# Hybrid trunk on one core: the carried state's product made in whole 128-row matmuls, its decay and the norm sums on VectorE, the last group's scaling moved

## The chip, the core and the metric

The kernel runs on one core of one Trainium2 chip. The time is that of one execution on the device, in microseconds (us). Three runs of the kernel before gave 1942.26, 1942.64 and 1945.34 us; the median, 1942.64 us, is the time that the change is measured against.

## The reference, cut to what matters

One layer of a decoder trunk over 1024 positions and 1024 channels: a normed input is projected, goes through a convolution branch and a state-space branch (SSD), is mixed, and passes a gated feed-forward part. The change lies in the state-space branch, in the norm of the convolution branch and in the order of the work between the two. For a chunk of 128 positions, and for each of 32 heads (8 to a group, 64 channels to a head), the branch computes:

```python
a_cs = cumsum(a)                                   # per head, over the chunk
decay = where(causal, exp(a_cs[l] - a_cs[s]), 0)
y_diag = (C @ B.T * decay) @ xs                    # inside the chunk
y_off  = (C @ carry) * exp(a_cs)                   # from the carried state
carry  = exp(a_cs[-1]) * carry + new_state
y = (y_diag + y_off + x * d_skip) * silu(z)
y = y * rsqrt(mean(y**2) + eps) * norm_w           # over the group's 512 channels
```

The convolution branch ends in a layer norm over 1024 channels (`mean`, then the mean of the squared differences), a scaling and a silu.

## The kernel before, in words

The sequence is taken in two halves of 512 positions (`hh` 0 and 1). Channels lie on the 128 partitions, positions along the free axis. A projection of 128 channels is 24 matmuls of 128x128 weights by 512 positions: eight blocks of the contraction, three products each, because each operand is held as a high and a low part (`project`, `mm3`, lines 189 to 204). ScalarE makes the high part of the weights by a cast (L158), VectorE the low part by a subtraction (L163); in the second half the low part of most weights comes back from memory instead (L160). The weights go through three buffers, so a cast waits for the product that used the buffer three products earlier.

`mixers(hh)` runs four groups `g`. For each group it projects and convolves B, C and x, projects the gate z, makes two products of the convolution branch, and then calls `ssd_group`, whose four chunks `c` are mixed into the projections that come next. A chunk, on its engines:

- SyncE loads `ab`: the eight heads' `a_cs`, each copied to all 128 partitions (L640).
- TensorE transposes x and B and multiplies B by C (L646 to L650).
- ScalarE makes the decay (`m`, L653 and L660) and `exp(a_cs)` for all eight heads (`ce`, 128x1024, L663). GpSimd multiplies `ce` by C (L664).
- VectorE masks the product of B and C (`cbm`), scales x to `xs` and `xsd`, and multiplies `m` by `cbm` (L680).
- TensorE adds up, for each head, `xs` times `m` (L685) and the state times `ce` (L688) in one bank `py`; each of these products fills 64 of the 128 output rows, and two heads share the rows. Then it makes the new state `pn` (L693).
- VectorE decays the state and adds the new one (L697, L700), adds the skip term (L703), multiplies by `zs` (L714); ScalarE squares, VectorE sums the squares (L717, L718).

`fill` places taps of a 31-tap convolution (L577, one VectorE instruction each, 480 in all) behind chosen instructions. `scaled()` turns the sum of squares of a finished group into a factor: a TensorE product (L725), a square root (L733), a reciprocal (L734), a small store and a load that copies the row to all partitions, both issued from GpSimd's queue (L736, L737), then four scalings of x (L740). `parts` splits the scaled x into high and low parts (ScalarE L754, VectorE L755). For groups 0 to 2 they are called while the next group is under way; for group 3 they stand inside the gate products `gate_first`, after number 4 of 0 to 7. Then `gated` follows with the eight `gb` products. `held` keeps the four scalings and ties them behind an instruction chosen by hand: the last skip of chunk 0 of the next group, or, for group 3, the low part of the first `gb` weights.

`conv_norm` loads the eight convolved blocks (L862), adds them up on GpSimd (L864, L866), subtracts the mean on VectorE, squares on ScalarE and adds the squares on GpSimd (L876). It runs once beside the `gated` products of the second half, for the first half's data, and once beside the products of `mixed`.

Names in the views: `acc` and `sm` are the two sets of four accumulation banks, `w_*` weights, `st_*` weights as loaded, `c_5`, `c_6` the convolution's sums, `x_1_3` the x of group 3 of the second half, `state_106` the state of group 3.

The order of instructions on each engine is fixed when the program is built: a scheduler places them by priorities and its own timing, and each engine then takes its list strictly in that order.

Of the kernel before, what the change touches and what calls it, by code (L numbers as in the profile page):

```python
# [8 lines left out]
F32 = mybir.dt.float32  # L9
F32R = mybir.dt.float32r  # L10
AF = mybir.ActivationFunctionType
# [52 lines left out]
def kernel(  # L64
# [557 lines left out]
    def ssd_group(pl, hh, g, xT, BT, CT, zs):  # L622
# [10 lines left out]
        for c in range(4):  # L633
# [25 lines left out]
                )  # L659
            exps.append(A.activation(out=m, in_=m, func=AF.Exp, scale=-1.0))  # L660
            if not first:
                ce = pl.tile([P, 8, P], F32, tag="ce", name=f"ce{nm}")
                A.activation(out=ce, in_=ab, func=AF.Exp)  # L663
                G.tensor_tensor(  # L664
                    out=ce, in0=ce, in1=CT[:, cs].unsqueeze(1).to_broadcast([P, 8, P]), op=ALU.mult
                )
            cbm = pl.tile([P, P], F32, tag="cbm", name=f"cbm{nm}")
            V.tensor_mul(cbm, pb[:, P : 2 * P], upper)
# [13 lines left out]
            for i in range(4):  # L682
                pair = [(2 * i + k, py[k * HP : (k + 1) * HP, i * P : (i + 1) * P]) for k in (0, 1)]
                for h, o in pair:
                    TE.matmul(o, xs[:, h * HP : (h + 1) * HP], m[:, h, :], start=True, stop=first)  # L685
                if not first:
                    for h, o in pair:
                        TE.matmul(  # L688
                            o, S[:, h * HP : (h + 1) * HP], ce[:, h, :], start=False, stop=True
                        )  # L690
            if not last:
                pn = bank(0)
                TE.matmul(pn, bt, xsd, start=True, stop=True)  # L693
# [7 lines left out]
            for i in range(4):  # L701
                k = PC_SD + 4 * g + i
                skip = V.scalar_tensor_tensor(  # L703
                    out=xT[:, i, cs],
                    in0=xT[:, i, cs],
                    scalar=pc[:, k : k + 1],
                    in1=py[:, i * P : (i + 1) * P],
                    op0=ALU.mult,
                    op1=ALU.add,
                )  # L710
            fill(FILL[hh][1], skip)
            while held and c == 0:
                issue_after(held.pop(), skip)
            V.tensor_mul(xT[:, :, cs], xT[:, :, cs], zs[:, :, cs])  # L714
            sq = pl.tile([P, 4, P], F32, tag="sq", name=f"sq{nm}")
# [62 lines left out]
    def mixers(hh, hT):  # L778
        pre = first_columns(hh, hT, (CT_B, CT_C, CT_X))
        with pool(f"mixers{hh}") as pl:  # L780
            time_steps(pl, hh, pre[0])
            scaled = parts = None
            for g in range(GROUPS):
                BT = conv4(pl, hh, column(hh, hT, CT_B + g) if g else pre[1], 16 + g)
                CT = conv4(pl, hh, column(hh, hT, CT_C + g) if g else pre[2], 20 + g)
                xT = pl.tile([P, 4, HALF], F32, tag="x4", bufs=2, name=f"x4_{hh}_{g}")
                for i in range(4):
                    j = 4 * g + i
                    conv4(pl, hh, column(hh, hT, CT_X + j) if j else pre[3], j, xT[:, i, :])
                zs = z_gate(pl, hh, hT, g)  # L790
                for i in (2 * g, 2 * g + 1):
                    glu(pl, hh, hT, i)
                    conv31(hh, i)
                if g:
                    scaled()
                if g == 1:
                    yT = big_tile(f"yT{hh}_0")
                if g in (1, 2):
                    parts(yT)
                split_2 = parts  # L800
                scaled, parts = ssd_group(pl, hh, g, xT, BT, CT, zs)
                if g == 3:
                    ssm_out_first(pl, hh, yT)
                    yT = big_tile(f"yT{hh}_2")
                    split_2(yT)
                    gate_first(pl, hh, hT, range(3))
            for j in range(3, 8):
                gate_first(pl, hh, hT, (j,))
                fill(FILL[hh][2], los[-1])
                if j == 4:  # L810
                    scaled()
                    parts(yT)
        return yT

    def gated(pl, hh, hT, yT, during):
# [37 lines left out]
    def conv_norm(pl, hh, place):  # L853

        squares = pl.tile([P, 2, HALF], F32, tag="sq", name=f"csq{hh}")
        stats = pl.tile([P, 2, HALF], F32, tag="stats", name=f"stats{hh}")
        mean, var = stats[:, 0, :], stats[:, 1, :]
        n = 8
        pairs = [pl.tile([P, 2, HALF], F32, tag=f"c{i}", name=f"cc{hh}_{i}") for i in range(n // 2)]
        cs = []  # L860
        for i in range(n):
            G.dma_start(pairs[i // 2][:, i % 2, :], c_scr[hh][i])  # L862
            cs.append(pairs[i // 2][:, i % 2, :])
        G.tensor_add(mean, cs[0], cs[1])  # L864
        for c in cs[2:]:
            G.tensor_add(mean, mean, c)  # L866
        pm = bank(0)
        TE.matmul(pm, mean_w, mean, start=True, stop=True)
        for i, c in enumerate(cs):
            V.tensor_tensor(out=c, in0=c, in1=pm, op=ALU.subtract)  # L870
            if i == 0:
                A.activation(out=var, in_=c, func=AF.Square)
            else:
                sq = squares[:, i % 2, :]
                A.activation(out=sq, in_=c, func=AF.Square)
                G.tensor_add(var, var, sq)  # L876
        return lambda: conv_silu(pl, cs, var, place)

    def conv_silu(pl, cs, var, place):
# [677 lines left out]
```

## Time and profile before

| | before |
|---|---|
| median of three runs | 1942.64 us |
| the profiled execution's own time | 1943.56 us |
| its span in the trace | 1941.9 us |
| TensorE (PE) busy | 1922.9 us, 99% |
| VectorE (DVE) busy | 1617.1 us, 83% |
| ScalarE (ACT) busy | 1099.7 us, 57% |
| GpSimd (POOL) busy | 227.2 us, 12% |

Rows of a timeline give the start in us from the span's start, the length in us, the engine, the line, the operation, what it writes and reads, how many instructions of that kind stand together, and in brackets how long the engine was idle before it and what ended that. Rows of the waits give who waited for whom, the total in us, how often, and the longest. A row of a line gives, behind the colon, the shortest, median and longest duration in ns. Matmuls overlap in the records: each of 512 columns is shown as 0.39 us long, but one starts every 0.23 us, so starts are what to read.

### The profile page before, as it was taken

The page shows a single profiled execution, that of the slowest core. Times are in us where ns is not written, and L with a number is a line of the kernel's source. Part 1 is how long each engine was busy: PE and PEld are TensorE (multiplying, and loading weights), DVE is VectorE, ACT ScalarE, POOL GpSimd, SP SyncE. Part 2 cuts the span into 40 slices and gives each one's busy share as a digit, 9 for nine tenths or more (in the row PEclk, how much of TensorE's full clock was granted, in tenths as well). Part 3 has the DMA queues.
Part 4 walks back from the last instruction along what each step waited for, and adds up shares of the span by engine and source line. Part 5 has one row for each costly group of instructions (what it writes and reads, how often), then busy time and mean ns, then how long its engine had stood idle before and what let it go on. Part 6 is the DMA issues. An engine that isn't in the chain of part 4 may idle for free.

```text
span 1941.9 us, 25994 instructions
## 1 busy us (share of the span) xinstructions
PE 1922.9 (99%) x9424; PEld 1570.9 (81%) x9424; DVE 1617.1 (83%) x2222; ACT 1099.7 (57%) x1628; POOL 227.2 (12%) x275
## 2 busy tenths in 40 slices
PE   9999999999999999999999999999999999999998
PEld 8878888888878888878777888888888888888886
DVE  7488989797998697999978797787788888888778
ACT  6585878654525777776543535365555555553534
POOL 1010011011000111111102250011000000022010
PEclk9999999999999999999999999999999999999999
DMA  6655555547586565564464465766445555479673
GB/s 229 217 193 202 205 201 184 174 160 262 201 286 206 199 215 206 197 217 172 165 226 159 161 229 185 254 250 238 156 163 196 174 178 186 161 275 357 206 245 115
DMA packets 138194, 398.44 MB, mean 205 GB/s; under 512 B 16432, under 2 KB 16976, under 8 KB 138064
## 3 DMA queue, kind: packets, MB, share of 16 engines
q1 hardware_dynamic: 116928, 335.39, 50.1%
q0 software_dynamic: 14656, 49.83, 7.1%
q10 hardware_dynamic: 6480, 11.55, 1.6%
q8 instruction: 74, 1.21, 0.2%
q14 instruction: 56, 0.46, 0.1%
HBM read 300.61 MB, written 96.09 MB: 204 GB/s over the span
## 4 chain that ended last, share of the span: by engine, by line
PE 77%; DVE 9%; issue 7%; DMA 4%; ACT 2%; POOL 1%; SPq 0%; DVEq 0%; POOLq 0%; ACTq 0%
PE acc L194 18%; PE acc L192 17%; PE acc L193 17%; PE sm L192 7%; PE sm L193 7%; PE sm L194 7%; DVE c L577 3%; DVE x L527 1%; PE acc L508 1%; PE sm L685 1%; DMA rstd<-nrm_scr 1%; PE sm L693 1%; ACT m L653 1%; POOL ce L664 1%; DMA w_c<-low_scr 1%
## 5 line engine op out<-in xcount | busy, mean ns | idle before, releaser
L192 PE MATMUL acc<-hT_h,w_c 128*128 128x512 f32 x1000 | 391.8, 392 | 0.0
L194 PE MATMUL acc<-hT_h,w_c 128*128 128x512 f32 x1000 | 390.5, 391 | 0.1
L193 PE MATMUL acc<-hT_l,w_c 128*128 128x512 f32 x1000 | 389.9, 390 | 0.0
L577 DVE SCALAR_TENSOR_TENSOR c<-vl,pc,c 128x512 f32<-128x512 f32 x480 | 374.4, 800 | 8.0 <-ACT c L566 3.6
L192 PEld LDWEIGHTS acc<-hT_h,w_c 128*128 128x128 f32 x1000 | 187.8, 188 | 40.8 <-issue 2.0
L194 PEld LDWEIGHTS acc<-hT_h,w_c 128*128 128x128 f32 x1000 | 187.8, 188 | 40.1 <-issue 0.8
L193 PEld LDWEIGHTS acc<-hT_l,w_c 128*128 128x128 f32 x1000 | 187.8, 188 | 38.9 <-issue 0.6
L158 ACT CAST w_c<-st_c 128x1024 fp32r<-128x1024 f32 x128 | 133.8, 1046 | 148.1 <-PE acc L194 88.5
L664 POOL TENSOR_TENSOR ce<-ce,xbc 128x1024 f32<-128x1024 f32 x28 | 77.7, 2776 | 489.2 <-ACT ce L663 489.2
L1282 ACT CAST w_dn<-dr 128x1024 fp32r<-128x1024 f32 (+1 forms) x72 | 67.1, 942 | 75.3 <-DVE dr L1215 39.6
L163 DVE TENSOR_TENSOR w_c<-st_c,w_c 128x1024 fp32r<-128x1024 f32 x62 | 76.9, 1242 | 36.9 <-ACT w_c L158 36.7
L192 PE MATMUL sm<-h1s,w_s 128*128 128x512 f32 x264 | 102.8, 389 | 0.5 <-ACT fuv L1125 0.5
L193 PE MATMUL sm<-h1s,w_s 128*128 128x512 f32 x264 | 102.7, 389 | 0.0
L194 PE MATMUL sm<-h1s,w_s 128*128 128x512 f32 x264 | 102.2, 389 | 0.0
L653 ACT ACTIVATE m<-ab,acs 128x128 f32<-128x128 f32 x256 | 78.5, 389 | 27.8 <-PE sm L685 26.0
L1283 DVE TENSOR_TENSOR w_dn<-dr,w_dn 128x1024 fp32r<-128x1024 f32 (+1 forms) x72 | 77.7, 1086 | 4.8 <-ACT w_dn L1282 4.6
L527 DVE SCALAR_TENSOR_TENSOR x<-u,pc,x 128x512 f32<-128x512 f32 x96 | 71.0, 753 | 2.7 <-ACT x L525 2.7
L194 PE MATMUL acc<-h1b_h,w_ue 128*128 128x512 f32 x176 | 68.6, 395 | 0.3 <-DVE w_ue L163 0.3
L192 PE MATMUL acc<-h1b_h,w_ue 128*128 128x512 f32 x176 | 68.7, 391 | 0.0
L193 PE MATMUL acc<-h1b_l,w_ue 128*128 128x512 f32 x176 | 68.6, 390 | 0.0
L192 PE MATMUL sm<-h1b_h,w_s 128*128 128x512 f32 x176 | 68.5, 389 | 0.0
L193 PE MATMUL sm<-h1b_l,w_s 128*128 128x512 f32 x176 | 68.5, 389 | 0.0
(369 smaller groups left out, 4592.7 us busy)
## 6 DMA issues: line engine op xcount, KB each, us to landing
st_c<-wcol SPq DMA_DIRECT2D x128, 512.0 KB, 4.5
low_scr<-w_c SPq DMA_DIRECT2D x64, 512.0 KB, 2.9
w_c<-low_scr SPq DMA_DIRECT2D x64, 512.0 KB, 4.4
ab<-acs_scr SPq DMA_DIRECT2D x32, 512.0 KB, 4.0
dr<-wdown SPq DMA_DIRECT2D x55, 256.0 KB, 5.1
st_wo<-wo SPq DMA_DIRECT2D x24, 512.0 KB, 4.1
st_ue<-wup SPq DMA_DIRECT2D x22, 512.0 KB, 3.8
first_scr<-first ACTq DMA_DIRECT2D x44, 256.0 KB, 3.0
```

The lines of the kernel that those rows point to most:

```text
L158: casts.append(A.copy(w[:, 0, :], st))
L163: sub.tensor_tensor(out=w[:, 1, :], in0=st, in1=w[:, 0, :].bitcast(F32), op=ALU.subtract)
L192: TE.matmul(ps, wa(0), xa(0), start=start, stop=False, skip_group_check=more)
L193: TE.matmul(ps, wa(0), xa(1), start=False, stop=False, skip_group_check=more)
L194: TE.matmul(ps, wa(1), xa(0), start=False, stop=stop, skip_group_check=more)
L508: mm = TE.matmul(pss[o][:, ts], ws[o][:, i, k * P : (k + 1) * P], hT[:, j, k, ts], start=n == 0 and k == 0, stop=n == 2 and k == KD - 1,)
L527: V.scalar_tensor_tensor(out=o, in0=u[:, k : k + HALF], scalar=pc[:, wc + k : wc + k + 1], in1=o, op0=ALU.mult, op1=ALU.add,)
L577: step = V.scalar_tensor_tensor(out=c, in0=v[:, k : k + HALF], scalar=pc[:, wc + k : wc + k + 1], in1=c, op0=ALU.mult, op1=ALU.add,)
L653: A.activation(out=m[:, h, :], in_=ab[:, h, :], func=AF.Relu, scale=-1.0, bias=acs[:, c, 8 * g + h : 8 * g + h + 1],)
L664: G.tensor_tensor(out=ce, in0=ce, in1=CT[:, cs].unsqueeze(1).to_broadcast([P, 8, P]), op=ALU.mult)
L1282: A.copy(w[:, 0, cs], src)
L1283: V.tensor_tensor(out=w[:, 1, cs], in0=src, in1=w[:, 0, cs].bitcast(F32), op=ALU.subtract)
```

## The change

1. The carried state's part of a chunk is no longer made head by head with the decay inside the moving operand. Four products of 128 state columns (two heads) by C go to a bank `pq` of their own, early in the chunk; `exp(a_cs)` is made at half the size (128x512, with the even heads' rows on partitions 0 to 63 and the odd heads' on 64 to 127, loaded by two more transfers), and VectorE multiplies `pq` by it. GpSimd's multiplication goes. The skip term takes the result (`ce`) as its addend, and one more VectorE addition brings in `py`.
2. The additions in `conv_norm` (7 for the mean, 7 for the squares, in each of two calls) go from GpSimd to VectorE.
3. For group 3, `scaled()` and `parts` are called two gate products earlier; the scalings of group 2 are tied behind chunk 2 of group 3 and no longer behind chunk 0.

```diff
             if not first:
-                ce = pl.tile([P, 8, P], F32, tag="ce", name=f"ce{nm}")
-                A.activation(out=ce, in_=ab, func=AF.Exp)
-                G.tensor_tensor(
-                    out=ce, in0=ce, in1=CT[:, cs].unsqueeze(1).to_broadcast([P, 8, P]), op=ALU.mult
+                ce = pl.tile([P, 4, P], F32, tag="ce", name=f"ce{nm}")
+                by_two = acs_scr[hh][r : r + 8, :].rearrange("(i k) l -> k i l", k=2)
+                for k in range(2):
+                    SY.dma_start(
+                        ce[k * HP : (k + 1) * HP], by_two[k].partition_broadcast(HP)
+                    )
+                A.activation(out=ce, in_=ce, func=AF.Exp)
+                pq = bank(0)
+                for i in range(4):
+                    TE.matmul(
+                        pq[:, i * P : (i + 1) * P], S[:, i * P : (i + 1) * P], CT[:, cs],
+                        start=True, stop=True,
+                    )
+                V.tensor_tensor(
+                    out=ce, in0=pq.rearrange("p (i l) -> p i l", i=4), in1=ce, op=ALU.mult
                 )
...
-                    TE.matmul(o, xs[:, h * HP : (h + 1) * HP], m[:, h, :], start=True, stop=first)
-                if not first:
-                    for h, o in pair:
-                        TE.matmul(
-                            o, S[:, h * HP : (h + 1) * HP], ce[:, h, :], start=False, stop=True
-                        )
+                    TE.matmul(o, xs[:, h * HP : (h + 1) * HP], m[:, h, :], start=True, stop=True)
...
-                    in1=py[:, i * P : (i + 1) * P],
+                    in1=py[:, i * P : (i + 1) * P] if first else ce[:, i],
...
+            if not first:
+                skip = V.tensor_tensor(
+                    out=xT[:, :, cs],
+                    in0=xT[:, :, cs],
+                    in1=py.rearrange("p (i l) -> p i l", i=4),
+                    op=ALU.add,
+                )
             fill(FILL[hh][1], skip)
-            while held and c == 0:
+            while held and c == (2 if g == 3 else 0):
...
                     gate_first(pl, hh, hT, range(3))
+                    scaled()
+                    parts(yT)
             for j in range(3, 8):
                 gate_first(pl, hh, hT, (j,))
                 fill(FILL[hh][2], los[-1])
-                if j == 4:
-                    scaled()
-                    parts(yT)
...
-        G.tensor_add(mean, cs[0], cs[1])
+        V.tensor_add(mean, cs[0], cs[1])
         for c in cs[2:]:
-            G.tensor_add(mean, mean, c)
+            V.tensor_add(mean, mean, c)
...
-                G.tensor_add(var, var, sq)
+                V.tensor_add(var, var, sq)
```

The lines of the changed kernel that the prediction names: the two loads of `ce` L665, its Exp L668, the products into `pq` L671, the multiplication by the decay L675, `m` times `cbm` L691, the products inside the chunk L696, the state's decay and addition L703 and L706, the skip term L709, the new addition of `py` L718, the scalings L753, the sums of `conv_norm` L876, L878 and L888.

How the instructions stand, at three places. First TensorE in the second half, group 3, chunk 2. Before, from the last two pairs of the chunk's products to the projection that follows:

```order
L685 MATMUL sm_8290<-m_3_2_8268,xs_3_2_8283 64x128 x2
L688 MATMUL sm_8290<-ce_3_2_8278,state_106 64x128 x2
L693 MATMUL sm_8307<-xsd_3_2_8285,bt_3_2_8287 128x512
L646 MATMUL sm_8331<-ident,x_1_3_7667 128x128 x4
L650 MATMUL sm_8336<-xbc_23_7659,xbc_19_7620 128x128
L192 MATMUL acc_8593<-yT_0_h,w_so_6_8590 128x512
```

Now the state's products stand 15 projection matmuls ahead of the others, between matmuls of an earlier projection (`w_so_4`):

```order
L193 MATMUL acc_8527<-yT_0_l,w_so_4_8524 128x512
L194 MATMUL acc_8527<-yT_0_h,w_so_4_8524 128x512
L671 MATMUL sm_8282<-xbc_23_7659,state_106 128x128 x4
L192 MATMUL acc_8527<-yT_0_h,w_so_4_8524 128x512
L193 MATMUL acc_8527<-yT_0_l,w_so_4_8524 128x512
```

and the chunk's own products come in one run, 21 projection matmuls earlier than before (in `w_so_5`, not `w_so_6`):

```order
L194 MATMUL acc_8560<-yT_0_h,w_so_5_8557 128x512
L696 MATMUL sm_8297<-m_3_2_8268,xs_3_2_8290 64x128 x8
L699 MATMUL sm_8306<-xsd_3_2_8292,bt_3_2_8294 128x512
L646 MATMUL sm_8331<-ident,x_1_3_7667 128x128 x4
L650 MATMUL sm_8336<-xbc_23_7659,xbc_19_7620 128x128
L192 MATMUL acc_8560<-yT_0_h,w_so_5_8557 128x512
```

TensorE now meets VectorE twice in a chunk: at L671, which needs the state, and at L696, which needs `m`.

Second, VectorE in the same group, from the state of chunk 1 to `m` of chunk 2. Before:

```order
L697 TENSOR_TENSOR state_106<-state_106,edc 128x512
L703 SCALAR_TENSOR_TENSOR x_1_3_7667<-x_1_3_7667,pc,sm_8220 128x128 x4
L577 SCALAR_TENSOR_TENSOR c_5_7581<-vl_5_7580,pc,c_5_7581 128x512
L700 TENSOR_TENSOR state_106<-state_106,sm_8237 128x512
L670 TENSOR_TENSOR xs_3_2_8283<-sm_8260,dtv 128x512
L675 TENSOR_TENSOR xsd_3_2_8285<-sm_8260,wds 128x512
L668 TENSOR_TENSOR cbm_3_2_8281<-sm_8265,upper 128x128
L714 TENSOR_TENSOR x_1_3_7667<-x_1_3_7667,zs_3_7820 128x4x128
L577 SCALAR_TENSOR_TENSOR c_5_7581<-vl_5_7580,pc,c_5_7581 128x512
L680 TENSOR_TENSOR m_3_2_8268<-m_3_2_8268,cbm_3_2_8281 128x1024
```

Now, up to the instruction ahead of `m`:

```order
L675 TENSOR_TENSOR ce_3_1_8208<-sm_8212,ce_3_1_8208 128x512
L703 TENSOR_TENSOR state_106<-state_106,edc 128x512
L577 SCALAR_TENSOR_TENSOR c_5_7581<-vl_5_7580,pc,c_5_7581 128x512
L709 SCALAR_TENSOR_TENSOR x_1_3_7667<-x_1_3_7667,pc,ce_3_1_8208 128x128 x4
L577 SCALAR_TENSOR_TENSOR c_5_7581<-vl_5_7580,pc,c_5_7581 128x512
L706 TENSOR_TENSOR state_106<-state_106,sm_8236 128x512
L718 TENSOR_TENSOR x_1_3_7667<-x_1_3_7667,sm_8227 128x4x128
L681 TENSOR_TENSOR xs_3_2_8290<-sm_8260,dtv 128x512
L686 TENSOR_TENSOR xsd_3_2_8292<-sm_8260,wds 128x512
L679 TENSOR_TENSOR cbm_3_2_8288<-sm_8265,upper 128x128
L577 SCALAR_TENSOR_TENSOR c_5_7581<-vl_5_7580,pc,c_5_7581 128x512
L727 TENSOR_TENSOR x_1_3_7667<-x_1_3_7667,zs_3_7820 128x4x128
```

The two added instructions, L675 and L718, stand in the chain between one chunk's state and the next chunk's `m`.

Third, VectorE at the end of the second half's mixers, where group 3 is scaled and the `gb` products begin. Before:

```order
L718 TENSOR_TENSOR ssum_3_8113<-sq_3_3_8386 128x128
L577 SCALAR_TENSOR_TENSOR c_6_8178<-vl_6_8177,pc,c_6_8178 128x512 x23
L734 RECIPROCAL rows_3_8838<-rows_3_8838 128x128
L163 TENSOR_TENSOR w_gb_0_8978<-st_gb_0_8976,w_gb_0_8978 128x1024
L740 SCALAR_TENSOR_TENSOR x_1_3_7667<-x_1_3_7667,pc,rstd_3_8837 128x512 x4
L755 TENSOR_TENSOR yT_2_l<-x_1_3_7667,yT_2_h 128x1024 x2
L163 TENSOR_TENSOR w_gb_1_9010<-st_gb_1_9008,w_gb_1_9010 128x1024
```

Now, from the taps ahead of the reciprocal:

```order
L577 SCALAR_TENSOR_TENSOR c_6_8178<-vl_6_8177,pc,c_6_8178 128x512 x4
L747 RECIPROCAL rows_3_8760<-rows_3_8760 128x128
L577 SCALAR_TENSOR_TENSOR c_6_8178<-vl_6_8177,pc,c_6_8178 128x512 x11
L163 TENSOR_TENSOR w_gb_0_8978<-st_gb_0_8976,w_gb_0_8978 128x1024
L753 SCALAR_TENSOR_TENSOR x_1_3_7667<-x_1_3_7667,pc,rstd_3_8759 128x512 x4
L768 TENSOR_TENSOR yT_2_l<-x_1_3_7667,yT_2_h 128x1024 x2
L163 TENSOR_TENSOR w_gb_1_9010<-st_gb_1_9008,w_gb_1_9010 128x1024
```

Eleven taps that stood ahead of the reciprocal now stand behind it; what follows the low part of `w_gb_0` is as before.

## The prediction

> **What bounds the kernel.** I read the page's first part, then the waits of TensorE, then the timelines of the places that they name. The page:
>
> ```profile
> span 1941.9 us, 25994 instructions
> ...
> PE 1922.9 (99%) x9424; PEld 1570.9 (81%) x9424; DVE 1617.1 (83%) x2222; ACT 1099.7 (57%) x1628; POOL 227.2 (12%) x275
> ```
>
> TensorE works 99% of the span. So only two things shorten the kernel: fewer TensorE steps, or less time in which TensorE waits or runs slowly. The table of its waits says how much is there:
>
> ```profile
> PE sm L685 <- DVE m L680: 3.5, 4, 1.4
> PE acc L194 <- DVE w_gb L163: 2.8, 1, 2.8
> PE sm L276 <- POOL ident masks.py:199: 1.7, 1, 1.7
> PE acc L192 <- DVE r L967: 1.1, 1, 1.1
> ```
>
> Totals, counts and longest. The first two lie in code that the change moves; the third is the start of the program, the fourth the part after the mixers, and neither is touched. TensorE's timeline around the second:
>
> ```profile
> 1028.41 0.39 PE L192 MATMUL acc<-hT_h,w_gb 128*128 128x512 f32 x1
> 1028.64 0.39 PE L193 MATMUL acc<-hT_l,w_gb 128*128 128x512 f32 x1
> 1031.86 0.50 PE L194 MATMUL acc<-hT_h,w_gb 128*128 128x512 f32 x1 [2.83 <-DVE w_gb L163]
> ...
> 1035.84 0.40 PE L192 MATMUL acc<-hT_h,w_gb 128*128 128x512 f32 x1
> ```
>
> A 512-column matmul starts every 0.23 us (1028.41 to 1028.64). From 1028.64 to 1035.84 there are 11 steps: 7.20 us where 11 x 0.23 = 2.5 would do. So this one place loses 4.7 us, not 2.8. The rest is the clock; the window just behind the wait (PE, PEld, DVE, ACT, POOL busy, then the granted clock, 0.57):
>
> ```profile
> 1031.90:1035.40 3.50, 3.50 (x9) 2.74 (x10) 3.43 (x3) 0.00 (x0) 3.34 (x3) 0.57 0.66 205
> ```
>
> **Part 1, the gate stall: -4.7.** VectorE's timeline ahead of it:
>
> ```profile
> 1009.52 0.95 DVE L734 RECIPROCAL rows<-rows 128x128 f32<-128x128 f32 x1 [0.59 <-ACT rows L733]
> 1013.38 1.23 DVE L163 TENSOR_TENSOR w_gb<-st_gb,w_gb 128x1024 fp32r<-128x1024 f32 x1 [2.91 <-ACT w_gb L158]
> 1021.34 3.78 DVE L740 SCALAR_TENSOR_TENSOR x<-x,pc,rstd 128x512 f32<-128x512 f32 x4 [6.73 <-DMA rstd<-nrm_scr]
> ...
> 1029.52 2.28 DVE L163 TENSOR_TENSOR w_gb<-st_gb,w_gb 128x1024 fp32r<-128x1024 f32 x1
> ```
>
> The low part of w_gb_1, for which TensorE waits, stands behind the scalings, and these waited 6.73 us for the factor. The factor takes 1021.34 - 1009.52 = 11.8 us from the reciprocal's start (store, load, both from GpSimd's queue). The change moves its TensorE product two gate products ahead: 48 matmuls x 0.23 = 11 us. On VectorE the reciprocal passes 11 taps, 11 x 0.75 = 8.2 us (the tap's row follows below), and that is the smaller, so it counts: start at 1001.3, factor at 1013.1. The scalings stand behind the low part of w_gb_0, which ends at 1014.6; the factor is there by then. From the scalings' start to the end of that last L163 passed 1031.8 - 1021.3 = 10.5 us, so w_gb_1 would be ready at 1025.1, against 1028.87 where TensorE wants it: 3.8 us to spare. Wait and slow clock both go.
>
> [...]
>
> **Part 2, the waits for m: -3.5.** VectorE and TensorE around the two longest:
>
> ```profile
> 964.25 5.92 DVE L577 SCALAR_TENSOR_TENSOR c<-vl,pc,c 128x512 f32<-128x512 f32 x5
> ...
> 973.64 0.68 DVE L670 TENSOR_TENSOR xs<-sm,dtv 128x512 f32<-128x512 f32 x1
> 974.24 0.28 DVE L668 TENSOR_TENSOR cbm<-sm,upper 128x128 f32<-128x128 f32 x1
> ...
> 976.37 1.21 DVE L680 TENSOR_TENSOR m<-m,cbm 128x1024 f32<-128x1024 f32 x1
> ```
>
> Five taps take 5.92 us, 2.2 over 5 x 0.75 (the median tap, below), and on GpSimd at that time:
>
> ```profile
> 966.75 2.86 POOL L664 TENSOR_TENSOR ce<-ce,xbc 128x1024 f32<-128x1024 f32 x1 [12.06 <-ACT ce L663]
> ```
>
> A VectorE instruction that meets the GpSimd multiplication lasts until this ends. The multiplication goes, and so should these waits.
>
> **Part 3, TensorE's work: +1.4.** A chunk before:
>
> ```profile
> 119.07 0.39 PE L688 MATMUL sm<-ce,state 128*64 128x128 f32 x4
> 119.29 0.39 PE L685 MATMUL sm<-m,xs 128*64 128x128 f32 x4
> ...
> 122.20 0.39 PE L650 MATMUL sm<-xbc,xbc 128*128 128x128 f32 x2
> 122.35 0.48 PE L192 MATMUL acc<-hT_h,w_c 128*128 128x512 f32 x1
> 122.66 0.40 PE L193 MATMUL acc<-hT_l,w_c 128*128 128x512 f32 x1
> ```
>
> The removed L688 came in four groups of 0.22 (119.07 to 119.29): 0.88 a chunk. Half-filled rows were not lost, since two heads ran at once. The added L671 are four products of the shape of L650, 128x128 by 128. From L650 to L193 pass 0.46 us, of which L192 has 0.23, so one product costs 0.23 and four 0.92. In 28 chunks (32, less the first of each group in the first half) that is 28 x 0.05 = 1.4 us more. TensorE's work does not shrink.
>
> **Part 4, VectorE in the chunks: nothing, of 0 to 14; 1.0 taken.** L675 and L718 each read a bank and write 512 columns, as the L670 at 973.64 does, behind which the next instruction starts 0.60 us later: 28 x 1.2 = 34 us more. The relief is read from a line's row (shortest, median, longest ns) and from the groups of the page with their means (800, 959):
>
> ```profile
> L577 DVE SCALAR_TENSOR_TENSOR c<-vl,pc,c x480: 653/746/2978, 108.7 to 1060.8; 128x512 f32<-128x512 f32 x160
> ```
>
> ```profile
> L577 DVE SCALAR_TENSOR_TENSOR c<-vl,pc,c 128x512 f32<-128x512 f32 x480 | 374.4, 800 | 8.0 <-ACT c L566 3.6
> ...
> L714 DVE TENSOR_TENSOR x<-x,zs 128x512 f32<-128x512 f32 x32 | 30.7, 959 | 0.0
> ```
>
> The taps' mean stands 54 ns over their median, 480 x 0.054 = 26 us; L714's 959 stands 0.28 over the 0.68 of an undisturbed instruction of its size, 32 x 0.28 = 9 us. Together 35 against 34: the sum is nought. But the relief falls wherever GpSimd's multiplication happened to fall, and the addition always between the state and m. That matters because VectorE is full there:
>
> ```profile
> 850.00:900.00 50.00, 50.00 (x293) 40.58 (x292) 49.57 (x81) 37.80 (x66) 6.28 (x3) 1.00 0.47 166
> ```
>
> and the room between m and TensorE's use of it can be small (VectorE, then TensorE):
>
> ```profile
> 885.30 1.21 DVE L680 TENSOR_TENSOR m<-m,cbm 128x1024 f32<-128x1024 f32 x1
> ```
>
> ```profile
> 886.71 0.44 PE L685 MATMUL sm<-m,xs 128*64 128x128 f32 x4
> ```
>
> m ends at 886.51, 0.2 us early. TensorE now also waits, at L671, for the state of the chunk before, and behind a late L671 or L696 all projections stand. How the two meetings lie to each other, by the order in group 3: TensorE takes 4 x 0.23 for L671 and 15 x 0.23 to L696, 4.4 us. VectorE, from the state's addition to m, has L718, xs, xsd and the scaling by zs at 0.60, cbm 0.28, a tap 0.75 and m 1.21, in all 4.6. So the lists are balanced to 0.2 us: whoever meets at L671 just in time meets at L696 just in time too. Bounds: a gain is excluded beyond the waits already counted, since TensorE has no others; on the other side half a microsecond (one added instruction without relief) in each of 28 chunks, 14 us. I take 1.0, near the low end: one wait of the present size (3.5 / 4 = 0.9), since 28 of the 32 chunks had none before, and the work is the same.
>
> **Part 5, at nothing.** ScalarE's Exp halves; ScalarE is at 57%. SyncE issues 56 more loads. `ce` has a single buffer, so load, Exp and L675 follow the skip L709 of the chunk before; a load of this kind lands after
>
> ```profile
> ab<-acs_scr SPq DMA_DIRECT2D x32, 512.0 KB, 4.0
> ```
>
> 4.0 us, and for the Exp of 512 columns I allow what VectorE needs for as many, 0.6: 4.6 in all. Behind L709 VectorE has, by the order, a tap, L706, L718, xs, xsd, cbm, a tap, the scaling by zs and m, 6.6 us, before it can come to the next L675. If that cover fails, L675 is late by the difference, and L709 and L718 with it; the state and m do not wait for it, other than in VectorE's queue. The 28 additions of `conv_norm` cost VectorE some 17 us by
>
> ```profile
> 1100.57 4.91 DVE L886 TENSOR_TENSOR cc<-cc,stats 128x512 f32<-128x512 f32 x8
> ```
>
> (0.61 each), beside products in which VectorE also loses its GpSimd neighbour. What hides them is that weights have three buffers and are made about two products ahead, 2 x 24 x 0.23 = 11 us; without that, a burst of 7 x 0.61 = 4.3 us would show at TensorE. GpSimd's own additions go; nobody waited for them in the rows above.
>
> **The sum.** Own time 1943.56 - 4.7 - 3.5 + 1.4 + 1.0 = 1937.8; it lay 0.9 above the median of the runs, so 1936.9. Its own range: 1934.0 (no new wait, products no dearer: -2.4, and 0.5 of scatter) to 1938.7 (0.1 us of wait a chunk, +1.8).
>
> **Rivals.** 0.2% is 3.9 us, about what a measurement of this kernel tells from no change: "same" is 1938.8 to 1946.5.
>
> A. *The gate stall stays.* The factor is late after all, by a slower store or load in GpSimd's queue, behind the eight loads of `conv_norm`, or the low part of w_gb_1 waits behind the additions now on VectorE. Against it: 3.8 us of room. 1936.9 + 4.7 = 1941.6, same. Chance 0.10.
>
> B. *A second meeting.* L671 needs the decayed and summed state of the chunk before, L696 needs m; each must be met. At 0.15 us a chunk, 28 x 0.15 = 4.2, so 1941.1, same (from 0.1 us a chunk on). For it: the 0.2 us of room above, and lists that are just balanced. Against: with one meeting a chunk only 4 of 32 chunks waited, and the worst two of these by the multiplication that goes. Chance 0.12.
>
> C. *VectorE becomes the bound in the chunks.* In the window above it is busy 49.57 of 50. If the relief does not fall between state and m, half the addition, 0.6 us a chunk, stops TensorE: 28 x 0.6 = 17, 1953.7, slower. It decides from (1946.5 - 1936.9) / 28 = 0.35 us a chunk. For it: both added instructions stand in that chain, and the waits for m show that TensorE stops as soon as VectorE slips 2 us. Against: three GpSimd multiplications stand in that same window, 6.28 us, and taps can lie behind. Chance 0.15.
>
> D. *The slow clock stays without the wait.* The 4.7 - 2.8 = 1.9 us behind the wait are not its consequence: 1936.9 + 1.9 = 1938.8, just same. Against: the slow stretch begins with the wait's end, and the clock is 1.00 in the window at 850. Chance 0.05.
>
> That the change is not what it says is out: the rows of the order show it.
>
> **Chances.** Forecast 0.58, A 0.10, B 0.12, C 0.15, D 0.05. Faster 0.58, same 0.27 (A, B, D), slower 0.15. The range runs from 1934.0 to 1943.5: it takes in A, B with waits up to 0.23 us a chunk, and D, and leaves C out.
>
> **What would show it.** Right: no wait for w_gb and a granted clock of 1.0 around 1030; L163's waits behind the scalings gone; the longest tap near 0.75 us in place of 2.98, its mean near 750; waits for m under 1 us in sum; POOL's busy time down by at least 28 x 2.86 = 80 us. Wrong: new waits "L671 <- state" or "L696 <- m" of over 5 us, or a wait of L194 for w_gb or w_co on VectorE, with TensorE's busy time as before.

## The result, and the profile after

The changed kernel takes 1940.16 us, the median of 22 runs (1938.09 to 1945.91); the kernel before, in as many runs beside it, 1943.2 us. The ratio is 0.9984 with an interval of 0.9977 to 0.9990: a gain of 3.0 us, which is under the 0.2% that the prediction called no change. The forecast was 1936.9 us with a gain of 5.7. The time lies in the stated range, the gain is about half the forecast one, and what came is "same" (chance 0.27), not the "faster" that the prediction held likelier (0.58).

The page of the changed kernel (span, then the share of each engine):

```profile
span 1939.3 us, 25653 instructions
...
PE 1924.2 (99%) x9200; PEld 1569.9 (81%) x9200; DVE 1603.8 (83%) x2306; ACT 1076.3 (55%) x1618; POOL 101.5 (5%) x219
```

VectorE is busy 13 us less although it has 84 more instructions; GpSimd lost 126 us. TensorE's waits (in total, times, longest):

```profile
PE sm L276 <- POOL ident masks.py:199: 1.7, 1, 1.7
PE sm L696 <- DVE m L691: 1.6, 1, 1.6
PE acc L192 <- DVE r L979: 1.1, 1, 1.1
...
PE sm L671 <- DVE state L706: 0.3, 1, 0.3
```

The wait for w_gb is gone, and so are the four waits for m where they were. In their place stands one wait for m near 747 us, which is new, and a small one for the state; m was to be waited for less than 1 us in sum, and this is the one sign of being right that did not come. The taps, in the page's group and the line's row (shortest, median, longest):

```profile
L577 DVE SCALAR_TENSOR_TENSOR c<-vl,pc,c 128x512 f32<-128x512 f32 x480 | 346.4, 744 | 4.6 <-ACT c L566 1.1
```

```profile
L577 DVE SCALAR_TENSOR_TENSOR c<-vl,pc,c x480: 652/744/755, 109.1 to 1054.3; 128x512 f32<-128x512 f32 x160
```

No tap is lengthened any more (755 ns at most, where 2978 was the longest). The gate on VectorE:

```profile
998.80 0.95 DVE L747 RECIPROCAL rows<-rows 128x128 f32<-128x128 f32 x1
...
1013.53 1.23 DVE L163 TENSOR_TENSOR w_gb<-st_gb,w_gb 128x1024 fp32r<-128x1024 f32 x1 [5.34 <-ACT w_gb L158]
1014.67 2.73 DVE L753 SCALAR_TENSOR_TENSOR x<-x,pc,rstd 128x512 f32<-128x512 f32 x4
1017.32 2.43 DVE L768 TENSOR_TENSOR yT_l<-x,yT_h 128x1024 fp32r<-128x1024 f32 x2
1019.66 1.22 DVE L163 TENSOR_TENSOR w_gb<-st_gb,w_gb 128x1024 fp32r<-128x1024 f32 x1
```

The scalings wait for nothing, and they, the low parts and the low weights take 6.2 us (1014.67 to 1020.88) where the same rows took 10.5 before. Both have changed, the start and the length; which of the two removed the stall, the experiments tell.

For the sums below I use one stretch of TensorE's records: from the start of the last of the first half's step products (L474, at 34 us) to the first product of `w_sp` in the second half. It holds all that the change moves but the second call of `conv_norm`, and behind `w_wo`, some 90 us later, the order on every engine is the same before and after. It is 1037.2 us before and 1032.2 us after. One run of those below, of the kernel with a third buffer for vl, took 5900 us; the median and the ratio of that kernel are given without it.

### The profile page after: what moved, and what is told of

Same layout as the page of the kernel before. It is cut to its first block, busy times and chain, and to the rows that moved or that the text cites. A ratio compares the mean times of both kernels' runs of the same rounds, so it can differ in the third digit from the quotient of the medians.

```text
span 1939.3 us, 25653 instructions
## 1 busy us (share of the span) xinstructions
PE 1924.2 (99%) x9200; PEld 1569.9 (81%) x9200; DVE 1603.8 (83%) x2306; ACT 1076.3 (55%) x1618; POOL 101.5 (5%) x219
## 3 DMA queue, kind: packets, MB, share of 16 engines
q8 instruction: 72, 1.18, 0.2%
## 4 chain that ended last, share of the span: by engine, by line
PE 88%; DMA 6%; DVE 4%; issue 1%; ACT 1%; SPq 0%; DVEq 0%; ACTq 0%; POOLq 0%
PE acc L194 22%; PE acc L192 21%; PE acc L193 21%; PE sm L193 5%; PE sm L192 5%; PE sm L194 5%; DMA dr<-wdown 2%; PE sm L696 2%; PE sm L699 1%; PE sm L671 1%; DVE w_dn L1295 1%; DMA dr<-b_scr 1%; PE acc L508 1%; DMA st_wo<-wo 1%; PE sm L646 1%
## 5 line engine op out<-in xcount | busy, mean ns | idle before, releaser
L577 DVE SCALAR_TENSOR_TENSOR c<-vl,pc,c 128x512 f32<-128x512 f32 x480 | 346.4, 744 | 4.6 <-ACT c L566 1.1
L192 PE MATMUL sm<-h1s,w_s 128*128 128x512 f32 x264 | 102.8, 390 | 0.5 <-ACT fuv L1137 0.5
L192 PE MATMUL sm<-h1b_h,w_s 128*128 128x512 f32 x176 | 68.5, 389 | 0.0
L194 PE MATMUL sm<-h1b_h,w_s 128*128 128x512 f32 x176 | 68.5, 389 | 0.0
```

The costliest lines, as they stand in the source:

```text
L192: TE.matmul(ps, wa(0), xa(0), start=start, stop=False, skip_group_check=more)
L194: TE.matmul(ps, wa(1), xa(0), start=False, stop=stop, skip_group_check=more)
L577: step = V.scalar_tensor_tensor(out=c, in0=v[:, k : k + HALF], scalar=pc[:, wc + k : wc + k + 1], in1=c, op0=ALU.mult, op1=ALU.add,)
```

## The experiments

| | median, us | ratio | interval | stretch, us |
|---|---|---|---|---|
| before, again | 1944.48 | 1.0000 | 0.9991 to 1.0009 | 1037.4 |
| changed, again | 1940.95 | 0.9978 | 0.9969 to 0.9987 | 1035.3 |
| gate calls alone | 1939.78 | 0.9982 | 0.9973 to 0.9991 | 1032.9 |
| norm additions alone | 1938.48 | 0.9968 | 0.9956 to 0.9979 | 1029.5 |
| state product alone | 1938.16 | 0.9971 | 0.9961 to 0.9980 | 1032.0 |
| before without GpSimd's multiplication | 1937.99 | 0.9965 | 0.9951 to 0.9978 | 1033.2 |
| changed, third part undone | 1937.05 | 0.9959 | 0.9946 to 0.9972 | 1031.9 |
| changed, third buffer for vl | 1941.14 | 0.9990 | 0.9978 to 1.0003 | 1034.6 |
| changed, two buffers for ce | 1939.60 | 0.9980 | 0.9972 to 0.9989 | 1032.7 |
| third part undone and two buffers for ce | 1939.85 | 0.9976 | 0.9966 to 0.9986 | 1032.1 |
| changed, only the tie undone | 1939.33 | 0.9982 | 0.9970 to 0.9994 | 1035.2 |
| changed without the addition of py | 1938.06 | 0.9966 | 0.9954 to 0.9977 | 1031.4 |

Each ratio is against runs of the kernel before on the same chip; the stretch is that of the one profiled execution, which is not always near the median: with the norm additions alone it was the fastest of six (1934.74 us), with the state product alone the slowest of nine (1941.07 us). Differences of a few us between stretches are therefore read together with the waits that make them.

**The gate calls alone.**

```diff
                     gate_first(pl, hh, hT, range(3))
+                    scaled()
+                    parts(yT)
...
-                if j == 4:
-                    scaled()
-                    parts(yT)
```

> Only the call of the scaling and the splitting of group 3 two gate products earlier; all else as before. Theory (the gate stall comes from the late factor): the wait of TensorE for w_gb and the slow clock behind it are gone, -4.7 us (ratio 0.9976); the waits for m stay at 3.5. Rival (the stall comes from GpSimd's additions, which lengthen the scalings, the low parts and the low weights on VectorE by some 4 us): a wait for w_gb of 1 us or more stays, and the gain is under 2 us. Rival D (the slow clock is not tied to the wait): a stretch at a granted clock near 0.57 stays, gain 2.8.

VectorE's timeline:

```profile
1014.10 1.23 DVE L163 TENSOR_TENSOR w_gb<-st_gb,w_gb 128x1024 fp32r<-128x1024 f32 x1 [4.21 <-ACT w_gb L158]
1015.24 6.88 DVE L740 SCALAR_TENSOR_TENSOR x<-x,pc,rstd 128x512 f32<-128x512 f32 x4
1022.04 4.56 DVE L755 TENSOR_TENSOR yT_l<-x,yT_h 128x1024 fp32r<-128x1024 f32 x2
1026.52 2.30 DVE L163 TENSOR_TENSOR w_gb<-st_gb,w_gb 128x1024 fp32r<-128x1024 f32 x1
```

and GpSimd's beside it:

```profile
1016.55 11.19 POOL L865 TENSOR_TENSOR stats<-stats,cc 128x512 f32<-128x512 f32 x6
```

The factor is in time and the stall is gone, with the slow clock (granted 1.00 from 1015 to 1030 us). But the chain takes 13.6 us (1015.24 to 1028.82) against 6.2 without GpSimd beside it. The next matmul of w_gb_1 on TensorE starts at 1028.90: the 3.8 us of room that the prediction worked out are all but used up, since GpSimd's additions are met by more of the chain than before. The waits for m stayed (4.2 in five).

**The norm additions alone.**

```diff
-        G.tensor_add(mean, cs[0], cs[1])
+        V.tensor_add(mean, cs[0], cs[1])
...
-                G.tensor_add(var, var, sq)
+                V.tensor_add(var, var, sq)
```

> Only the additions of the convolution's norm on VectorE instead of GpSimd. By the theory of the late factor alone the scalings still start near 1021.3 and still wait over 6 us, and the wait for w_gb of 2.8 stays: 0. By the rival (lengthened instructions) scalings, low parts and the low weights take 2.7 + 2.4 + 1.2 = 6.4 us instead of 10.5, w_gb_1 is ready at 1027.6 against 1028.9, and the stall goes though the factor is as late as before: -4.7. If the additions cost TensorE something where they now stand, a new wait on w_gb, w_sp or w_co shows there, up to 4.3.

```profile
1015.89 2.74 DVE L740 SCALAR_TENSOR_TENSOR x<-x,pc,rstd 128x512 f32<-128x512 f32 x4 [4.35 <-DMA rstd<-nrm_scr]
1018.55 2.43 DVE L755 TENSOR_TENSOR yT_l<-x,yT_h 128x1024 fp32r<-128x1024 f32 x2
1020.90 1.22 DVE L163 TENSOR_TENSOR w_gb<-st_gb,w_gb 128x1024 fp32r<-128x1024 f32 x1
```

Here the factor is late (VectorE waits 4.35 us for it), and TensorE still has no wait: the lengthened instructions were as much the cause as the late factor, and either half removes the stall alone. The 28 additions cost TensorE no wait where they now stand. The waits for m fell too, from 3.5 to 1.1; GpSimd's multiplications are still there, but the order on VectorE around them is another. That this order is the reason is read from the rows, not tested by itself. It is the shortest stretch of all, 7.7 us under before, in an execution that was 3.7 us under this kernel's median.

**The state product alone.** The edit is the first part of the diff, without the others.

> Only the state's product in whole 128-row matmuls and its decay on VectorE; gate, norm additions and the tie of the scalings as before. Theory: TensorE's own work +1.3, the waits for m (3.5) go, new waits near 2 us come instead, the gate stall of 4.7 stays: in all 0, within 2 us. Rival (VectorE has relief to spare): waits for m and state under 0.5 in sum, -2. Rival C (VectorE is the bound): over +4.

In the profile no wait for m or the state stands in the table any more, and two for w_gb, 1.4 us in all, at full clock (1.00 from 1031 to 1036 us). The new waits near 2 us that I expected did not come, so on these the rival was right. The stretch is 5.2 us shorter, more than either expected, because the gate stall shrank with it: the low weights of w_gb_1 start earlier, between the two low parts.

**Before without the multiplication.**

```diff
                 A.activation(out=ce, in_=ab, func=AF.Exp)
-                G.tensor_tensor(
-                    out=ce, in0=ce, in1=CT[:, cs].unsqueeze(1).to_broadcast([P, 8, P]), op=ALU.mult
-                )
```

> The kernel before with GpSimd's multiplication of the decay by C left out (so the carried state's part is not the reference's), nothing added in its place. Theory (the multiplication holds VectorE): the waits of TensorE for m fall from 3.5 to under 0.7, no tap in the chunks takes over 0.8 us, -3 us; the gate stall stays. Rival (the waits for m come from the order on VectorE, not from GpSimd): they stay at 2 us or more, and the time is within 1 us of before.

TensorE's waits:

```profile
PE acc L194 <- DVE w_gb L163: 2.4, 1, 2.4
...
PE sm L682 <- DVE m L677: 0.4, 1, 0.4
```

m is waited for 0.4 us instead of 3.5, and VectorE's busy time falls by 40 us (1617.1 to 1577.2) with not one VectorE instruction less. So the multiplication held VectorE, and the relief of 35 us that the prediction took from means and medians was close.

**Both kernels again.** No edit.

> The changed kernel as it is, once more, for a second profile. Theory (what the first profile's sum left open is execution scatter behind the mixers, where the order is the same as before): the stretch from the first product of the second half's state projection back to the start repeats within 1 us, with the same waits for m (1.6) and the state (0.3), while the stretch from the last down-projection's first product to the end (218.4 us in the first profile, 216.0 before) comes out different by 1 us or more. Rival (the change lengthens the end itself): that stretch is over 218 again.

> The kernel before as it is, once more, for a second profile. Theory (scatter): gate stall of 4.7 and waits for m of 3.5 as in the first profile, within 0.5; the stretch of the down-projection to the end differs from 216.0 by up to 2 us. Rival (the stretches at the end belong to the kernel): 216.0 again, within 0.3.

My theory that the stretch repeats, and that only what lies behind it scatters, fell. Before repeats: stretch 1037.2 and 1037.4, waits for m 3.5 and 3.3, for w_gb 2.8 and 2.9. The changed kernel does not: 1032.2 and 1035.3. What lies behind the stretch takes 870.6 and 870.7 us in the two profiles of before, 872.7 and 871.5 in those of the changed kernel, and 869.6 to 873.0 in all fourteen profiles, in no order that follows the edits: I read that part as scatter. The second profile's waits:

```profile
PE sm L696 <- DVE m L691: 2.2, 1, 2.2
...
PE sm L649 <- DVE ce L675: 0.7, 1, 0.7
```

and two windows behind the wait at 747 (TensorE's clock is the number ahead of the DMA share, 0.68 and 0.63):

```profile
750.00:752.80 2.80, 2.58 (x18) 1.61 (x19) 2.73 (x8) 1.30 (x5) 0.56 (x1) 0.68 0.16 55
752.80:755.00 2.20, 2.20 (x10) 1.69 (x9) 1.16 (x2) 2.18 (x5) 0.00 (x0) 0.63 0.97 310
```

The new wait was 2.2 us here, not 1.6, and the clock fell behind it: the trace grants half of it for 3.41 us, from 751.03, which costs 1.7 us. The chain that ends in it, in the first profile, on ScalarE:

```profile
742.09 0.82 ACT L566 ACTIVATE c<-vl,pc 128x512 f32<-128x512 f32 x1 [9.64 <-DMA vl<-v_scr]
742.81 1.03 ACT L158 CAST w_c<-st_c 128x1024 fp32r<-128x1024 f32 x1
743.75 0.59 ACT L547 ACTIVATE v<-acc 128x512 f32<-128x512 f32 x1
744.35 1.28 ACT L746 ACT_TABLE_LOAD   x1
745.65 0.37 ACT L746 ACTIVATE rows<-sm,eps 128x128 f32<-128x128 f32 x1
```

on VectorE:

```profile
714.22 19.96 DVE L577 SCALAR_TENSOR_TENSOR c<-vl,pc,c 128x512 f32<-128x512 f32 x30
734.10 0.68 DVE L548 TENSOR_TENSOR v<-acc,v 128x512 f32<-128x512 f32 x1
734.70 2.19 DVE L577 SCALAR_TENSOR_TENSOR c<-vl,pc,c 128x512 f32<-128x512 f32 x3
...
744.37 0.69 DVE L548 TENSOR_TENSOR v<-acc,v 128x512 f32<-128x512 f32 x1 [5.15 <-ACT v L547]
746.05 0.95 DVE L747 RECIPROCAL rows<-rows 128x128 f32<-128x128 f32 x1 [0.99 <-ACT rows L746]
746.92 0.63 DVE L675 TENSOR_TENSOR ce<-sm,ce 128x512 f32<-128x512 f32 x1
747.46 0.68 DVE L703 TENSOR_TENSOR state<-state,edc 128x512 f32<-128x512 f32 x1
748.06 1.22 DVE L691 TENSOR_TENSOR m<-m,cbm 128x1024 f32<-128x1024 f32 x1
```

and on TensorE:

```profile
749.42 0.84 PE L696 MATMUL sm<-m,xs 128*64 128x128 f32 x11 [1.62 <-DVE m L691]
```

Read from the bottom: m is late because VectorE, which takes its list in order, stands idle 5.15 us before L548 and 0.99 us before the reciprocal, both times for ScalarE (L547 and the square root); ScalarE had waited 9.64 us for the rows of the next convolution (vl), whose load can start only when the last tap of an earlier one is done. Three taps now end at 736.9. Before, the last tap of this place ended at 730.4, ScalarE's wait was shorter, and m followed the reciprocal at once:

```profile
736.05 0.81 ACT L566 ACTIVATE c<-vl,pc 128x512 f32<-128x512 f32 x1 [4.17 <-DMA vl<-v_scr]
```

```profile
740.00 0.95 DVE L734 RECIPROCAL rows<-rows 128x128 f32<-128x128 f32 x1 [0.76 <-ACT rows L733]
740.88 1.16 DVE L680 TENSOR_TENSOR m<-m,cbm 128x1024 f32<-128x1024 f32 x1
```

The chain from the load on is rigid: in all seven profiles in which TensorE waits for m here, its product L696 starts 7.33 or 7.34 us after ScalarE's L566, wherever that lies between 740.86 and 744.96. So each microsecond by which L566 starts later comes out at the product. Of the 7.33 us, 1.1 are L675 and the state's decay L703, which now stand between the reciprocal and m, so VectorE's work is in the wait directly too. How much of the wait each of the two makes was not separated, and why the taps end later in one execution than in another (736.9 and 737.5 in the two profiles) stays open.

**The third part undone.** State product and norm additions as in the change, the calls and the tie as before.

> The changed kernel with the third part undone (group 3 scaled and split in its old place, the tie of group 2's scalings at chunk 0); state product and norm additions as in the change. Theory (either the earlier factor or the freed VectorE removes the gate stall alone): no wait for w_gb over 0.3, full clock; as fast as the changed kernel or up to 2 us faster, since the order around the scalings is that of before. Rival (the gate move is needed): a wait for w_gb of 1 us or more.

No wait for w_gb: the gate move isn't needed. At 747 the waits are 0.6 for m and, later, 0.4 for the state. It is faster than before. Against the changed kernel, its interval (0.9946 to 0.9972) lies below that of the first runs (0.9977 to 0.9990) but touches that of the repeat on the same chip (0.9969 to 0.9987); there four of its five runs are shorter than all ten of the changed kernel's, 1937.05 against 1940.95 us by the medians. So it looks faster than the changed kernel too, on five runs.

**A third buffer for vl.**

```diff
-            v = statep.tile([P, HALF + KC - 1], F32, tag="v", bufs=2, name=f"vl{hh}_{i}")
+            v = statep.tile([P, HALF + KC - 1], F32, tag="v", bufs=3, name=f"vl{hh}_{i}")
```

> The changed kernel with a third buffer for the convolution's loaded rows (vl), so that the next load does not wait for the last tap. Theory (the new waits at 747 and 759 come from ScalarE, held 9.6 us by the start of a convolution, L566, whose rows are loaded late): no wait for m there, none at L671, the time 2 us below the changed kernel's. Rival (VectorE's two added instructions are the cause): the waits stay, 1.5 us or more in sum.

The waits for m stayed, 4.0 us in three, as the rival said. But ScalarE now waits for the other buffer of the convolution, its sum `c`, which must be stored first:

```profile
744.96 0.82 ACT L566 ACTIVATE c<-vl,pc 128x512 f32<-128x512 f32 x1 [9.23 <-DMA c_scr<-c]
```

So the edit moved ScalarE's wait and tested neither the theory nor the rival. Three buffers for both were not tried.

**Two buffers for ce.**

```diff
-                ce = pl.tile([P, 4, P], F32, tag="ce", name=f"ce{nm}")
+                ce = pl.tile([P, 4, P], F32, tag="ce", bufs=2, name=f"ce{nm}")
```

> The changed kernel with two buffers for ce; the order on TensorE and VectorE is the same to the row, only ScalarE's Exp and the two loads come earlier. Theory (the load of ce into its one buffer holds ScalarE, and through it m and L675): ScalarE's idle time before L668 falls from 26 to 32 us (two profiles) to under 5, the wait at L649 for ce near 951 is gone, the wait for m near 747 shrinks or stays (its cause is the late start of a convolution), and the time is 1 to 3 us below the changed kernel's. Rival (VectorE's added instructions): no change in the waits of TensorE, within 0.5 us of the changed kernel.

ScalarE's idle time before L668:

```profile
  DMA ce<-acs_scr: 26.8, 16
```

as much as without the second buffer (25.8 in 13 waits in the first profile). The load is late for other reasons than its buffer, and this theory falls. The wait for m near 747 is 0.6 us here, one of 1.3 stands at 119, and the time is that of the changed kernel.

**The third part undone and two buffers for ce.** The two edits above together.

> State product and norm additions as in the change, the third part undone, and two buffers for ce. Theory: no gate stall (VectorE is free of GpSimd's additions), waits of TensorE for m, state and ce under 1 us in sum, 1935 to 1937 us, 7 us or more below before. Rival (ce's buffer is nothing): the same as without it, 1937.

Its wait near 747 was 1.5 us in the profiled execution, and it was no faster than without the second buffer; the intervals of the two just overlap (0.9966 to 0.9972). Nor was it faster than the changed kernel with two buffers for ce on the same chip (1939.85 against 1939.60 us). So the gain of leaving the third part out, which the five runs above show, did not come again here.

**Only the tie undone.**

```diff
-            while held and c == (2 if g == 3 else 0):
+            while held and c == 0:
```

> The changed kernel with only the tie of the scalings put back to chunk 0 in every group; the earlier call for group 3 stays. Theory (what makes the changed kernel slower than the one with its third part undone is the earlier call in the first half, which leaves taps for later, so that the convolution before 747 ends later): wait for m of 1.5 us or more near 747, time within 1 us of the changed kernel's. Rival (the tie costs): that wait under 1 us, time near 1937.

Wait for m of 1.9 us near 747, the clock down behind it, the time that of the changed kernel: the tie is not it. What is left of the third part is the earlier call, in both halves; that this makes the taps before 747 end later is read from the rows (the last one ends at 735.3 us with the third part undone, at 736.9 and 737.5 in the changed kernel), and one row speaks against it: with the third part undone and two buffers for ce it ends at 736.9 as well. It stays open.

**Without the addition of py.**

```diff
-            if not first:
-                skip = V.tensor_tensor(
-                    out=xT[:, :, cs], in0=xT[:, :, cs],
-                    in1=py.rearrange("p (i l) -> p i l", i=4), op=ALU.add,
-                )
```

> The changed kernel without the new addition of py (L718 left out, so the part inside the chunk is missing from the result): 28 VectorE instructions, 17 us, fewer. Theory (the new waits come through ScalarE, which is held by loads): a wait for m of 1 us or more near 747 stays, ScalarE still waits over 15 us for ce, time 0 to 2 us below the changed kernel's. Rival C (VectorE's added work makes the new waits): waits for m, state and ce under 0.5 us in sum, time 3 us or more below.

TensorE's wait for m, and ScalarE at the place of the new wait:

```profile
PE sm L696 <- DVE m L691: 0.5, 2, 0.3
```

```profile
736.46 0.81 ACT L566 ACTIVATE c<-vl,pc 128x512 f32<-128x512 f32 x1 [3.66 <-DMA vl<-v_scr]
```

With 17 us of VectorE work fewer, the taps end earlier (the last at 726.1 us, not 736.9), ScalarE waits 3.66 us instead of 9.64, and the wait near 747 is gone; 0.7 us are left for m and the state in sum. The median is 2.9 us under the changed kernel's second one, on another chip; the intervals of the two overlap. So the rival was right that VectorE's added work makes the wait, and my theory right in the path, through a convolution that ends late and ScalarE's queue. ScalarE's wait for ce stayed at 26 us and did no harm.

## Why the prediction was half right

That the time lies in the range is in part luck: the range reached up to 1943.5 to take in rivals A, B and D, none of which came as priced, and the stretch of the two profiles fell by 5.0 and 2.0 us. Terms as forecast, and as the two profiles of the changed kernel have them, from the stretch:

- **Gate stall, -4.7:** gone in both. But it had two causes of which the prediction saw one. Part 1 took the 10.5 us from the scalings to the low weights as fixed; 4.3 of them were GpSimd's additions. With these on VectorE, the third part of the change had nothing left to remove. The earlier calls alone remove the stall too, but with 0.08 us to spare and not 3.8.
- **Slow clock (rival D):** where the stall went, the slow clock went too (granted 1.00 from 1015 to 1030 us with the gate calls alone, from 1031 to 1036 with the state product alone, and from 36 to 1060 in the first profile of the changed kernel), and it came back behind the new wait in the second profile; it belonged to the wait. It does not begin with the wait's end, as rival D has it, but 0.55 us later (half clock from 1032.41 us, the wait's end at 1031.86).
- **Waits for m, -3.5:** gone where they were. Leaving out the multiplication alone takes them to 0.4, so it makes most of them; but with it in place they fell to 1.1 in the kernel with the norm additions alone, so the order around it counts too. Part 2's sentence that a VectorE instruction lasts until the multiplication ends is too wide: of the 30 taps beside a GpSimd addition or multiplication in the kernel before, 15 were not lengthened (0.73 to 0.75 us).
- **TensorE's work, +1.4:** +1.7. The chunks' own rows in the stretch shrank from 104.5 to 102.8 us, but the projections are interrupted once more in a chunk, and the steps from one projection matmul to the next lose 3.4 us (10.8 us over 0.2267 a step, against 7.4 in the kernel with the norm additions alone, which has no stall).
- **New waits, +1.0:** this is the step that failed. The first profile has 1.8 at m and 0.5 at the state by the matmuls' starts, 2.3 in all; the stretch of the second is another 3.1 us longer, with a longer wait, one for ce, one for bt (the copy L690), and the clock down behind it: 1.3 us more of waits, and 1.9 more in the chunks' own rows, of which the half clock makes 1.7. So 2.3 to 5.4.

The sum for the first profile: -5.2 for the gate (the projections' excess of 12.6 against 7.4) - 3.8 for m by starts + 1.7 + 2.3 = -5.0, and the stretch says -5.0. For the second -2.0. The medians of whole executions, -3.0 and -3.4, lie between.

Part 4 was wrong not in its arithmetic of VectorE (34 added in the chunks, 35 of relief; the taps' mean fell to the median) but in where it looked: it weighed the two meetings L671 and L696 in one chunk, and there the lists do balance. What it left out is what stands behind the taps. A tap that is put off puts off the next convolution's load, and ScalarE, which Part 5 waved through at 57%, stood 9.6 us before that load, with L547 and the square root behind it that VectorE needs ahead of m. (Part 5's cover of 6.6 us adds up to 6.0 by its own rows; it still stands over the 4.6 of the load and the Exp. Even so ScalarE waited 25.8 us for ce in the first profile, which no run shows to have cost time.) Rival B (L671) was named as a second place of waiting and was not it: 0.3 us. Rival C had the right engine and the wrong place; it came to 2 to 5 us, not 17. (Both are priced on top of the 1.0 that the sum already takes for such waits; by that B is 1.0 too high, which leaves it "same".)

The calls for group 3, which the forecast credited with 4.7 us, remove nothing beside the norm additions. Without the third part the kernel was faster in one pair of kernels (1937.05 against 1940.95 us) and not in the other (1939.85 against 1939.60). State product and norm additions together give 0.9959, the norm additions alone 0.9968, the state product alone 0.9971; the intervals of these three overlap, and which is best stays open.

## What to carry to other kernels

When two edits of one change aim at the same stall, price the second with the first in place: the gate calls and the norm additions each remove the whole stall alone, and it can go only once. (The two without the state product were not run together.) A wait's row names the last releaser; before moving it, see whether the instructions between it and the waiting engine are lengthened. And where work is added to an engine that also runs filler, follow the filler: what is put off there, which load waits for that, and which queue stands before the load.

## What the runs showed of the hardware

Beside a GpSimd addition or multiplication, some VectorE instructions on SBUF operands took longer: four scalings 6.88 us with the gate calls alone against 2.73 in the changed kernel, two low parts 4.56 against 2.43. Of the 30 taps beside one in the kernel before, 15 took 1.65 to 2.98 us and end 0.55 us behind the end of a GpSimd instruction that they met; the other 15 took 0.73 to 0.75 us, and 14 of these had begun ahead of GpSimd's instruction, against two of the lengthened ones, by 0.02 and 0.03 us. The state's addition L700, which reads a bank, ran beside one seven times and was not lengthened (671 to 683 ns, where all 24 take 670 to 683).

The clock was halved (granted 0.50) in the kernel before for 3.41 us, from 0.55 us behind the end of a TensorE wait of 2.83 us. It fell, too, behind waits of 2.15 us (the changed kernel's second profile: 0.68 and 0.63 in the windows shown, from 0.81 us behind the wait's end), of 1.85 us (only the tie undone: 0.77 from 751 to 754 us and 0.60 from there to 756.5) and of 2.4 us (before without the multiplication: 0.62 from 1033.5 to 1037.5 us). (These, and the 0.57 of the prediction's window, are means that take in some full speed as well.) It stayed at 1.00 behind waits of 1.62 us (the changed kernel's first profile, 749.4 to 755 us), 1.18 and 1.75 us (state product alone, 1033.5 to 1036 and 1350.4 to 1354 us). Behind a wait of 2.12 us (third buffer for vl) the new state's product L699 took 1.12 us, as L693 did at 120.70 in the kernel before; behind the wait of 2.15 it took 2.08. That 1.85 slowed and 2.12 did not says that the length alone does not set it.
